# A decoder layer with 32 experts: weight reads in longer pieces, a 2 MB ring, the first token tile ahead, and a reordered tail

## The chip, the cores and the metric

The kernel runs on one core of one Trainium2 chip. The metric is device time in microseconds (us) of that core; lower is better. Several runs are taken and the median counts.

## What is computed

One layer of a hybrid decoder on 256 tokens of 1024 channels, in float32: a token mixer (gated delta rule, a linear recurrent unit and sliding-window attention, merged and projected), then 32 experts of which each token takes its top four, then a gated per-token embedding, with a layer norm after each.

```python
def moe(h, router_w, router_b, w_gu, b_gu, w_down, b_down):
    logits = (xt @ router_w + router_b).astype(jnp.float32)
    top_vals, top_idx = lax.top_k(logits, TOP_K)            # 4 of 32
    gates = jax.nn.softmax(top_vals, axis=-1)
    ...
        return clamped_swiglu(xb @ w_gu[e] + b_gu[e]) @ w_down[e] + b_down[e]
    ...

def reference(...):
        y = token_mixer(x, ...)                             # ends in (g_a*y_a + g_b*y_b + g_c*y_c) @ w_out
        x = layer_norm(DEEPNORM_ALPHA * x + y, ln1_g[i], ln1_b[i])
        y = moe(x, router_w[i], router_b[i], w_gu[i], b_gu[i], w_down[i], b_down[i])
        x = layer_norm(DEEPNORM_ALPHA * x + y, ln2_g[i], ln2_b[i])
        ple = jax.nn.sigmoid(x @ ple_w_gate[i]) * (p[i] @ ple_w_proj[i])
        x = layer_norm(DEEPNORM_ALPHA * x + ple, ln3_g[i], ln3_b[i])
```

`w_gu` is 1024 x 2048 per expert (8 MB), `w_down` 1024 x 1024 (4 MB): 384 MB in all, read once.

## The kernel before, in words

**Mixer** (to about 456 us). The work of TensorE is a list of *units*: a projection of 128 columns, or, at the end, `out_unit(c, t)`, the output projection of 256 columns (quarter `c`) for 128 tokens (tile `t`). Operands are split into a high and a low part, and a product is three matmuls (L350, L1085). Everything else (gates, recurrences, attention, norms) is written as generators, the *strands*; `run()` advances each by one `yield` per unit, and a strand may `wait` for named events. So the place of a `yield` and the order of the units set the order of instructions on each engine. After its last quarter a tile of tokens gets `first_norm(t)`: two scalar-tensor-tensor instructions per half of 512 channels (L1109, L1110), eight transposes on TensorE (L1115), copies on ScalarE, and the router's matmuls (L1122). `router()` then takes the top four per token on VectorE (L1146 to L1165), and turns them into positions.

**Experts** (`moe`). For each expert SyncE streams weights into a ring of buffers: 20 of 1 MB (8 KB per partition), of which the last eight lie in a pool `el` that the mixer shares, and are filled with the first expert's `w_gu` while the mixer ends (`prefetch`, L1037). `chunk` (L1288) reads one block of 128 rows of `w_gu`, `chunk3` (L1296) two blocks of `w_down`. A read is issued when TensorE has used up the buffer's former content. TensorE gathers the tokens of two experts at a time with one-hot matrices (`gathered`, L1358), multiplies with `w_gu` in eight steps over k (L1395, eight records a step), then VectorE and ScalarE do the clamped SwiGLU, TensorE turns it (L1423) and multiplies with `w_down` (L1431), and `spread` (L1454, L1459) adds the weighted result of the expert before to the accumulator `Y`. `mid(k)` and `fill(i)` place this other work between the steps. In expert 0 `mid` also places `residual()` (L1309): the sum of the gates times `b_down`, by two transposes (L1313) and eight matmul records (L1319), and the scaled residual as the first content of `Y`.

**Tail.** A branch for experts with more than 64 tokens (`overflow`), the second norm, the gate of the embedding (8 products over k of high and low parts, L1605, with weights split by `highs` on ScalarE and `lows` on VectorE or GpSimd, L1575), the sigmoid and product, the third norm, and the output. `moments` has a power on GpSimd (L1584) between the two instructions of a norm (L1588, L1589).

Names in the rows: `w`, `E` ring buffers, `xs` the normed tokens, `gu`, `dn`, `cb`, `pg`, `pjt` results in PSUM, `oh` one-hot matrices, `bd` and `gT` the down biases and turned gates, `mvs` mean and variance.

Of the kernel before, what the change touches and what calls it, by code (L numbers as in the profile page):

```python
# [27 lines left out]
RING = 20  # L28
EARLY = 8
# [82 lines left out]
def mixer(mx, tc, nc, a, xs, rt, dram, cst, ones, el):  # L112
# [32 lines left out]
    E = [el.tile([P, 2048], F32, name=f"E{i}", tag=f"E{i}") for i in range(4)]  # L145
# [54 lines left out]
    wg = big("E6", [P, 2, H, P])  # L200
# [4 lines left out]
    def late_parameters():  # L205
# [217 lines left out]
    M["BH"] = big("E4", [P, KD, T], F32R)  # L423
    M["BL"] = big("E5", [P, KD, T], F32R)
# [504 lines left out]
    def attend(gq, qT):  # L929
# [175 lines left out]
    def first_norm(t):  # L1105
        xT, gb = M["xT"], M["gb"]
        for hf in range(2):
            c = slice(hf * 512, (hf + 1) * 512)
            dve.scalar_tensor_tensor(xs[:, t, c], xs[:, t, c], mv[:, t, 0:1], gb[:, 0, c], ALU.subtract, ALU.mult)  # L1109
            dve.scalar_tensor_tensor(xs[:, t, c], xs[:, t, c], mv[:, t, 2:3], gb[:, 1, c], ALU.mult, ALU.add)  # L1110
        yield
        for hf in range(2):
# [5 lines left out]
            if t == 0:  # L1118
                yield
        for hf in range(2):  # L1120
            for k in range(4 * hf, 4 * hf + 4):
                pe.matmul(M["rps", t][:, :NE], xT[:, k, t * P:(t + 1) * P], rw[:, k], start=k == 0, stop=k == KD - 1)  # L1122
            if t == 0:
                yield
        yield
        events.add(f"r{t}")

    def router():

        yield from wait("r0")  # L1130
# [88 lines left out]
    for n, (t, c) in enumerate(((0, 0), (1, 0), (0, 1), (1, 1), (0, 2), (0, 3), (1, 2), (1, 3))):  # L1219
        units.append((*out_unit(c, t), (), n == 0))  # L1220
# [31 lines left out]
def moe(ctx, tc, nc, a, out, dbg, xs, rt, dram, cst, ones, el, early):  # L1252
# [53 lines left out]
    bd = w2.tile([NE, D], F32, name="bd", tag="xe")  # L1306
    pool.dma_start(bd, a["b_down"][0])

    def residual():  # L1309
        gT = w2.tile([NE, T], F32, name="gT", tag="gt")  # L1310
# [5 lines left out]
        for t in range(2):  # L1316
            for hf in range(2):
# [379 lines left out]
```

## Time and profile before

| | us |
|---|---|
| median of 3 runs (1451.98 to 1454.62) | 1453.3 |
| profiled execution | 1452.93 |
| its span, first to last instruction | 1451.2 |
| TensorE busy in the span | 1351.8 (93%) |
| VectorE, ScalarE, GpSimd busy | 608.7, 374.1, 258.9 |
| DMA: mean over the span | 332 GB/s |

The mean granted clock of TensorE is 0.981 of full speed. Busy times are sums over stages that differ, so they don't tell which engine sets the end of one; the rows below are read stage by stage.

### The profile page before, as it was taken

Reading aid. Unit: us, or ns where it says so; the run is one execution under the profiler, and the core shown is the slowest. Engines: PE = TensorE matmul, PEld = TensorE weight load, DVE = VectorE, ACT = ScalarE, POOL = GpSimd, SP = SyncE. Lnnn points to the kernel's source line nnn. Section 1 sums busy time; section 2 is a strip of 40 time slices with the busy share of each in tenths; the row PEclk is TensorE's granted clock in tenths of the full one; section 3 lists DMA queues with packets and bytes.
Section 4 is the critical chain, followed back from the end, with each engine's and each line's share of the span. In section 5 each row is a group of like instructions: output and inputs, shape, how many; then the busy total and the mean of one; then the engine's idle time right before and its main releaser. Section 6 shows DMA issues by size and latency. Waiting matters only on the chain. (4 is left out here: it accounts for less than half of the span.)

```text
span 1451.2 us, 21242 instructions
## 1 busy us (share of the span) xinstructions
PE 1351.8 (93%) x8472; PEld 781.2 (54%) x8473; DVE 608.7 (42%) x1285; ACT 374.1 (26%) x771; POOL 258.9 (18%) x221
## 2 busy tenths in 40 slices
PE   8989988999988999999999999999998989989976
PEld 7989988899988433333333333333333333333325
DVE  6497984965685222322322322222223222222257
ACT  6767464644551110110110111010101100101121
POOL 5655773534551000000000000000000000000021
PEclk9999999999998899999999999999999999999998
DMA  8754565446988699999999999999999999999960
GB/s 259 217 141 124 147 175 152 117 137 201 282 266 335 239 414 423 424 426 424 425 424 425 425 425 423 424 425 425 424 423 425 425 425 423 424 425 424 425 283 30
DMA packets 206832, 481.81 MB, mean 332 GB/s; under 512 B 13468, under 2 KB 137004, under 8 KB 174856
## 3 DMA queue, kind: packets, MB, share of 16 engines
q1 hardware_dynamic: 205128, 477.17, 84.7%
q0 software_dynamic: 848, 1.86, 0.4%
q10 hardware_dynamic: 752, 1.38, 0.3%
q8 instruction: 68, 1.11, 0.3%
q14 instruction: 36, 0.29, 0.1%
HBM read 478.78 MB, written 3.42 MB: 332 GB/s over the span
## 5 line engine op out<-in xcount | busy, mean ns | idle before, releaser
L1395 PE MATMUL gu<-w,xe 128*64 128x512 f32 x1208 | 274.8, 599 | 10.8 <-DMA w<-in_w_gu_dram 10.7
L350 PE MATMUL pjt<-xh,HI 128*128 128x256 f32 x680 | 199.0, 293 | 12.3 <-DVE cv L416 6.1
L1395 PE MATMUL gu<-E,xe 128*64 128x512 f32 x840 | 193.2, 603 | 6.7 <-DMA E<-in_w_gu_dram 6.7
L374 POOL TENSOR_TENSOR LO<-w,HI 128x384 fp32r<-128x384 f32 (+1 forms) x111 | 166.5, 1502 | 173.0 <-ACT HI L369 167.6
L350 PE MATMUL pjt<-xh,LO 128*128 128x256 f32 x680 | 193.1, 284 | 2.8 <-DVE LO L372 1.9
L350 PE MATMUL pjt<-xl,HI 128*128 128x256 f32 x680 | 193.0, 284 | 0.0
L1395 PEld LDWEIGHTS gu<-w,xe 128*64 128x64 f32 x1208 | 82.9, 137 | 177.4 <-issue 138.5
L1413 DVE TENSOR_SCALAR gc<-gu 128x256 f32<-128x256 f32 x64 | 26.9, 421 | 289.2 <-PE gu L1395 289.2
L1327 POOL DMA_DIRECT2D pt<-in_p_dram x1 | 0.8, 777 | 798.6 <-DVE lc L1417 798.6
L1431 PE MATMUL dn<-w,hT 128*64 128x512 f32 x608 | 140.5, 602 | 1.5 <-ACT hT L1424 1.5
L350 PEld LDWEIGHTS pjt<-xh,HI 128*128 128x128 f32 x680 | 130.8, 192 | 17.7 <-issue 4.3
L372 DVE TENSOR_TENSOR LO<-w,HI 128x640 fp32r<-128x640 f32 (+1 forms) x111 | 113.1, 1020 | 61.6 <-ACT HI L369 59.8
L350 PEld LDWEIGHTS pjt<-xh,LO 128*128 128x128 f32 x680 | 130.9, 192 | 3.2 <-DVE LO L372 2.1
L1459 DVE TENSOR_TENSOR Y<-Y,cb 128x512 f32<-128x512 f32 x128 | 82.1, 682 | 117.0 <-PE cb L1454 117.0
L350 PEld LDWEIGHTS pjt<-xl,HI 128*128 128x128 f32 x680 | 131.0, 193 | 0.2
L369 ACT CAST HI<-w 128x1024 fp32r<-128x1024 f32 x111 | 115.5, 1041 | 44.7 <-PE pjt L350 18.4
L1395 PEld LDWEIGHTS gu<-E,xe 128*64 128x64 f32 x840 | 57.6, 138 | 122.2 <-issue 97.9
L1414 ACT ACTIVATE sg<-gc 128x256 f32<-128x256 f32 x64 | 26.8, 419 | 298.2 <-DVE gc L1413 298.2
L1358 PE MATMUL gat<-oh,xs 128*128 128x128 f32 x512 | 75.9, 293 | 25.9 <-DVE oh L1366 19.9
L1431 PE MATMUL dn<-E,hT 128*64 128x512 f32 x416 | 95.4, 598 | 0.0
L1358 PEld LDWEIGHTS gat<-oh,xs 128*128 128x128 f32 x512 | 64.0, 196 | 47.1 <-issue 27.8
L1431 PEld LDWEIGHTS dn<-w,hT 128*64 128x64 f32 x608 | 40.4, 137 | 75.9 <-issue 64.4
(409 smaller groups left out, 1601.3 us busy)
## 6 DMA issues: line engine op xcount, KB each, us to landing
w<-in_w_gu_dram SPq DMA_DIRECT2D x151, 1024.0 KB, 19.6
E<-in_w_gu_dram SPq DMA_DIRECT2D x97, 1024.0 KB, 19.6
w<-in_w_down_dram SPq DMA_DIRECT2D x76, 1024.0 KB, 19.6
E<-in_w_down_dram SPq DMA_DIRECT2D x52, 1024.0 KB, 19.7
w<-in_w_in_dram SPq DMA_DIRECT2D x85, 512.0 KB, 3.8
E<-in_w_gu_dram SPq DMA_DIRECT2D x16, 512.0 KB, 4.8
w<-in_w_o_lru_dram SPq DMA_DIRECT2D x8, 512.0 KB, 4.6
w<-in_w_o_swa_dram SPq DMA_DIRECT2D x8, 512.0 KB, 3.9
```

Source lines behind the costliest of these rows:

```text
L350: pe.matmul(ps, hl[l][:, k], b[r][:, k], start=k == 0 and n == 0, stop=k == KD - 1 and n == 2)
L369: act.copy(hi, s)
L372: dve.tensor_sub(lo[:, 0:n], s[:, 0:n], hi[:, 0:n].bitcast(F32))
L374: pool.tensor_tensor(out=lo[:, n:], in0=s[:, n:], in1=hi[:, n:].bitcast(F32), op=ALU.subtract)
L1327: pool.dma_start(pt, a["p"][0, 0].rearrange("(t p) c -> p t c", p=P))
L1358: pe.matmul(ps[:, kk], xs[:, t, k * P:(k + 1) * P], oh[:, t], start=t == 0, stop=t == 1)
L1395: pe.matmul(gu[64 * j:64 * j + 64, b], xe[:, k], w[:, j * D + b * 512:j * D + (b + 1) * 512], start=False, stop=k == KD - 1)
L1413: dve.tensor_scalar(gc[:, c], guv[:, c, 0], 7.0, None, op0=ALU.min)
L1414: act.activation(sg[:, c], gc[:, c], AF.Sigmoid, scale=1.702)
L1431: pe.matmul(dn[64 * jj:64 * jj + 64], hT[:, 2 * hf + kk, j * 64:j * 64 + 64], w[:, kk, jj * 512:(jj + 1) * 512], start=hf == j == kk == 0, ...
L1459: dve.tensor_add(y, y, pss[jj])
```

## The change

Five things change together; line numbers in this section are those of the changed kernel where its code is meant.

1. **Layout and ring.** `w_gu` is read as "(p k) c": partition p holds rows 8p to 8p+7, so one read of 2 MB takes 16 KB in one piece per partition, with 64 KB from one partition's piece to the next. `w_down` is read as "(j h p c) d": 8 KB in one piece per partition, 1 MB per read, two reads per buffer. The ring has 10 buffers of 2 MB (16 KB per partition); four of them are prefetched. To match, the norm writes the channels of `xs` in another order (its second instruction reads with a stride of 8 elements), the router's weights are read in that order, and the turns of the SwiGLU's output take every second column. The first `spread` into each tile undoes the order, and brings the scaled residual in.
2. **Down biases** are added to `Y` in expert 22 instead of expert 0.
3. **Output projection.** Tile 0's quarters come earlier, its router matmuls stand together, and its top four are issued on VectorE behind the second tile's norm.
4. **Tail.** The gate's weights are issued from the last step of expert 31. GpSimd keeps one half block of the low parts, and VectorE does the rest. Norms are written as both first halves, then both second halves. The gate's products come in the order high-high, low-high, high-low.
5. `spread` takes its three products in another order.

```diff
-RING = 20
-EARLY = 8
+RING = 10
+EARLY = 4
...
-        for i in (0, 1, 2, 4, 5, 3, 6, 7):
...
-            t = el.tile([P, 2048], F32, name=f"E{i}", tag=f"E{i}")
...
-                sync.dma_start(t[:, c], a["w_gu"][0, 0, k * P:(k + 1) * P, c])
+        wgu = a["w_gu"][0, 0].rearrange("(p k) c -> p k c", k=KD)
+        for k, i in enumerate((0, 2, 1, 3)):
...
+            for n in range(2):
+                sync.dma_start(F[i][:, n * 2048:(n + 1) * 2048], wgu[:, 2 * k + n])
+                yield
                 yield
...
+        xc = wp.tile([P, KD, P], F32, name="xc", tag="w").rearrange("p a c -> p (a c)")
         for hf in range(2):
             c = slice(hf * 512, (hf + 1) * 512)
-            dve.scalar_tensor_tensor(xs[:, t, c], xs[:, t, c], mv[:, t, 0:1], gb[:, 0, c], ALU.subtract, ALU.mult)
-            dve.scalar_tensor_tensor(xs[:, t, c], xs[:, t, c], mv[:, t, 2:3], gb[:, 1, c], ALU.mult, ALU.add)
-        yield
+            dve.scalar_tensor_tensor(xc[:, c], xs[:, t, c], mv[:, t, 0:1], gb[:, 0, c], ALU.subtract, ALU.mult)
+        qk = lambda v, hf: v.rearrange("p (k q) -> p q k", q=KD)[:, 4 * hf:4 * hf + 4]
+        for hf in range(2):
+            dve.scalar_tensor_tensor(xs[:, t, 512 * hf:512 * hf + 512].rearrange("p (q k) -> p q k", q=4), qk(xc, hf),
+                                     mv[:, t, 2:3], qk(gb[:, 1], hf), ALU.mult, ALU.add)
...
-        yield from wait("r0")
+        yield from wait("r0", "n1")
...
-    for n, (t, c) in enumerate(((0, 0), (1, 0), (0, 1), (1, 1), (0, 2), (0, 3), (1, 2), (1, 3))):
+    for n, (t, c) in enumerate(((0, 0), (0, 1), (1, 0), (0, 2), (0, 3), (1, 1), (1, 2), (1, 3))):
...
+    def rows_up(src):
...
+                    units[k // 2] = buffer()
+                    sync.dma_start(units[k // 2], src(k // 2))
+            return units[k // 2][:, (k % 2) * 2048:(k % 2 + 1) * 2048]
...
+    def rows_down(src):
...
+                units[hf] = buffer()
+                for j2 in range(2):
+                    sync.dma_start(units[hf][:, j2 * 2048:(j2 + 1) * 2048], src(j2, hf))
...
-                dve.scalar_tensor_tensor(Y[:, t, sl], xs[:, t, sl], ALPHA, ps, ALU.mult, ALU.add)
...
+                dve.tensor_add(Y[:, t, sl], Y[:, t, sl], ps)
+                yield
...
-    wgu = a["w_gu"][0].rearrange("e (k p) c -> e k p c", p=P)
-    wdn = a["w_down"][0].rearrange("e (k p) c -> e p k c", p=P)
+    wgu = a["w_gu"][0].rearrange("e (p k) c -> e p (k c)", k=KD)
+    wdn = a["w_down"][0].rearrange("e (j h p c) d -> e j h p (c d)", j=2, h=2, c=2)
...
+                if t in fresh:
...
+                    dve.scalar_tensor_tensor(kq(y), xs[:, t].rearrange("p (q k) -> p q k", q=KD)[:, :, 64 * jj:64 * jj + 64],
+                                             ALPHA, kq(pss[jj]), ALU.mult, ALU.add)
...
-                if k == 1:
-                    next(begin)
-                if k == 3:
-                    next(begin)
-                if k == 4:
-                    next(begin, None)
+            if e == BIASED:
+                if k == 0:
+                    bias_rows.append(down_biases())
+                if k in (1, 3, 4, 5, 6):
+                    next(bias_rows[0])
...
-    lows(0, pool, slice(0, 1))
-    moments(0, 0, 2)
-    lows(0, pool, slice(1, 2))
-    for c in halves:
-        norm(0, 0, c)
...
-    lows(1, dve)
...
-    lows(2, pool)
...
-    lows(3, dve)
...
+    highs(0)
+    lows(0, pool, slice(0, 1))
     overflow()
...
+    moments(0, 0)
+    centred(0, 0, halves[0])
+    stats(1, 0)
+    scaled(0, 0, halves[0])
...
+    lows(0, dve, slice(1, 2))
+    for i in (1, 2, 3):
+        lows(i, dve)
...
+    gate(g0, 0, halves, "hl", True, False)
...
+    gate(g0, 0, halves, "w", False, True)
```

How it moves instructions, at three places. First PE at the end of the mixer, before: after the last unit come tile 0's transposes and a part of its router matmuls, between them the bias matmuls of expert 0 (L1379), then tile 1's transposes and the remaining router matmuls of both.

```order
L1115 MATMUL pg<-cst,xs 128x128 x8
L1379 LDWEIGHTS pick
L1379 MATMUL gu<-bias,pick 64x512
L1122 MATMUL pg<-rw,MG 128x32 x4
L1379 LDWEIGHTS pick
L1379 MATMUL gu<-bias,pick 64x512
L1379 LDWEIGHTS pick
L1379 MATMUL gu<-bias,pick 64x512
L1379 LDWEIGHTS pick
L1379 MATMUL gu<-bias,pick 64x512
L1115 MATMUL pg<-cst,xs 128x128 x8
L1122 MATMUL pg<-rw,MG 128x32 x12
```
PE there in the changed kernel, where the second to last unit ends and the last begins:

```order
L1091 MATMUL pjt<-RV,U 128x256
L1091 MATMUL pjt<-KT,AT 128x256
L1129 MATMUL pg<-cst,xs 128x128 x8
L1091 MATMUL pjt<-xh,AT 128x256
L1091 MATMUL pjt<-xh,U 128x256
```
and behind the last unit:

```order
L1091 MATMUL pjt<-xl,AT 128x256
L1135 MATMUL pg<-rw,MG 128x32 x8
L1403 LDWEIGHTS pick
L1403 MATMUL gu<-bias,pick 64x512
L1403 LDWEIGHTS pick
L1403 MATMUL gu<-bias,pick 64x512
L1403 LDWEIGHTS pick
L1403 MATMUL gu<-bias,pick 64x512
L1403 LDWEIGHTS pick
L1403 MATMUL gu<-bias,pick 64x512
L1129 MATMUL pg<-cst,xs 128x128 x8
L1135 MATMUL pg<-rw,MG 128x32 x8
```
Tile 0's transposes (L1129) now stand ahead of the last unit, and its router matmuls (L1135) ahead of tile 1's transposes; only tile 1's own follow.

Second, PE in the first expert, before (`E_` and `w_` with a number are ring buffers):

```order
L1358 MATMUL gat<-oh_5584,xs 128x128 x4
L1395 MATMUL gu<-E_4173,xe 64x512 x4
L1358 MATMUL gat<-oh_5584,xs 128x128 x4
L1313 MATMUL gps<-cst,GP 32x128 x2
L1395 MATMUL gu<-E_4260,xe 64x512 x4
L1401 MATMUL gwt<-cst,gw 128x128 x2
L1395 MATMUL gu<-E_4489,xe 64x512 x4
L1319 MATMUL cb<-bd,gT 128x512 x3
L1395 MATMUL gu<-E_4560,xe 64x512 x4
L1319 MATMUL cb<-bd,gT 128x512
L1395 MATMUL gu<-E_4703,xe 64x512 x4
L1395 MATMUL gu<-E_4778,xe 64x512 x4
```
and in the changed kernel:

```order
L1419 MATMUL gu<-F_97,xe 64x512 x4
L1382 MATMUL gat<-oh_5558,xs 128x128 x4
L1419 MATMUL gu<-F_97,xe 64x512 x4
L1382 MATMUL gat<-oh_5558,xs 128x128 x4
L1419 MATMUL gu<-F_4473,xe 64x512 x4
L1425 MATMUL gwt<-cst,gw 128x128 x2
L1419 MATMUL gu<-F_4473,xe 64x512 x4
L1419 MATMUL gu<-F_98,xe 64x512 x8
L1419 MATMUL gu<-F_99,xe 64x512 x8
```
L1313 and L1319 are gone from here, and two steps over k use one buffer.

Third, DVE in the tail, from tile 0's second norm on, before:

```order
L1582 BN_AGGR mvs<-bns 128x2
L1583 TENSOR_SCALAR mvs<-mvs 128x1
L1588 SCALAR_TENSOR_TENSOR Y<-Y,mvs,w_7495 128x512
L1589 SCALAR_TENSOR_TENSOR Y<-Y,mvs,w_7495 128x512
L1588 SCALAR_TENSOR_TENSOR Y<-Y,mvs,w_7495 128x512
L1589 SCALAR_TENSOR_TENSOR Y<-Y,mvs,w_7495 128x512
L1598 TENSOR_TENSOR w_10572<-tr,w_10571 128x4x128
L1575 TENSOR_TENSOR E_10303<-w_10294,E_10302 128x2048
L1598 TENSOR_TENSOR w_10572<-tr,w_10571 128x4x128
L1575 TENSOR_TENSOR E_10307<-w_10298,E_10306 128x2048
L1578 BN_STATS bns<-Y 128x6 x2
L1582 BN_AGGR mvs<-bns 128x2
```
and in the changed kernel, from the same norm's second instruction on:

```order
L1635 SCALAR_TENSOR_TENSOR Y<-Y,mvs,w_7330 128x512
L1632 SCALAR_TENSOR_TENSOR Y<-Y,mvs,w_7330 128x512
L1635 SCALAR_TENSOR_TENSOR Y<-Y,mvs,w_7330 128x512
L1623 BN_STATS bns<-Y 128x6
L1627 BN_AGGR mvs<-bns 128x2
L1628 TENSOR_SCALAR mvs<-mvs 128x1
L1645 TENSOR_TENSOR w_10215<-tr,w_10215 128x4x128 x2
L1632 SCALAR_TENSOR_TENSOR Y<-Y,mvs,w_7330 128x512 x2
L1635 SCALAR_TENSOR_TENSOR Y<-Y,mvs,w_7330 128x512 x2
L1620 TENSOR_TENSOR F_9898<-w_9890,F_9896 128x1024
L1620 TENSOR_TENSOR F_9898<-w_9890,F_9896 128x2048
L1620 TENSOR_TENSOR w_9899<-F_9893,F_9897 128x2048 x2
```
Tile 1's statistics and moments move up into tile 0's norm, its norm goes ahead of the subtractions of low parts (L1620), and there are three and a half blocks of these on DVE where there were two (L1575).

## Rows read from the trace of the kernel before

**Rows 1.** The page, parts 1 and 2: busy time; GB/s in 40 slices

```profile
PE 1351.8 (93%) x8472; PEld 781.2 (54%) x8473; DVE 608.7 (42%) x1285; ACT 374.1 (26%) x771; POOL 258.9 (18%) x221
...
GB/s 259 217 141 124 147 175 152 117 137 201 282 266 335 239 414 423 424 426 424 425 424 425 425 425 423 424 425 425 424 423 425 425 425 423 424 425 424 425 283 30
```

**Rows 2.** Stretches: PE, PEld, DVE, ACT, POOL busy, then clock, DMA share, GB/s

```profile
470.00:480.00 10.00, 9.69 (x49) 6.22 (x50) 2.17 (x13) 1.29 (x4) 0.56 (x1) 0.78 0.27 84
480.00:490.00 10.00, 10.00 (x40) 3.44 (x38) 2.48 (x4) 2.28 (x4) 0.00 (x0) 0.90 0.94 344
490.00:500.00 10.00, 7.86 (x32) 2.44 (x29) 2.92 (x8) 0.42 (x1) 0.00 (x0) 0.93 0.80 291
500.00:510.00 10.00, 9.29 (x44) 4.46 (x44) 1.29 (x4) 1.71 (x5) 0.00 (x0) 0.83 0.61 238
510.00:520.00 10.00, 10.00 (x52) 3.35 (x48) 1.63 (x4) 0.96 (x2) 0.00 (x0) 1.00 0.98 383
```

**Rows 3.** Timeline of SP's queue: start, duration, issue, count

```profile
476.62 8.73 SPq L1298 DMA_DIRECT2D E<-in_w_down_dram  x4
```

**Rows 4.** One line's instructions, L1401 on PE, in 540:900 and in 1130:1400

```profile
L1401 PE MATMUL gwt<-cst,gw x26: 272/300/328, 544.4 to 878.3; 128*128 128x128 f32 x26
...
L1401 PE MATMUL gwt<-cst,gw x18: 272/300/329, 1136.6 to 1379.0; 128*128 128x128 f32 x18
```

**Rows 5.** DMA traffic in 668.6:676.1 (w_down alone) and in 678.7:695.7 (w_gu alone)

```profile
DMA packets 817, 3.15 MB, mean 420 GB/s; under 512 B 49, under 2 KB 49, under 8 KB 816
...
DMA packets 993, 7.24 MB, mean 426 GB/s; under 512 B 110, under 2 KB 110, under 8 KB 110
```

**Rows 6.** Timeline of PE, the first expert and the start of the second

```profile
474.64 1.94 PE L1395 MATMUL gu<-E,xe 128*64 128x512 f32 x8
...
477.60 1.94 PE L1395 MATMUL gu<-E,xe 128*64 128x512 f32 x8
...
480.46 0.38 PE L1313 MATMUL gps<-cst,GP 128*32 128x128 f32 x2
480.77 1.94 PE L1395 MATMUL gu<-E,xe 128*64 128x512 f32 x8
...
484.88 2.84 PE L1319 MATMUL cb<-bd,gT 32*128 32x512 f32 x6
487.64 3.34 PE L1395 MATMUL gu<-E,xe 128*64 128x512 f32 x8
...
512.43 5.32 PE L1395 MATMUL gu<-w,xe 128*64 128x512 f32 x24
```

**Rows 7.** Timelines of PE, then DVE, at the end of the mixer

```profile
455.15 1.03 PE L1115 MATMUL pg<-cst,xs 128*128 128x128 f32 x8
...
460.64 5.08 PE L1122 MATMUL pg<-rw,MG 128*128 128x32 f32 x24
...
465.76 0.19 DVE L1146 TENSOR_TENSOR wk<-pg,small 128x32 f32<-128x32 f32 x1 [5.73 <-PE pg L1122]
...
468.38 0.18 DVE L1146 TENSOR_TENSOR wk<-pg,small 128x32 f32<-128x32 f32 x1
```

**Rows 8.** Timelines of DVE, then POOL, in the tail

```profile
1408.01 2.83 DVE L1589 SCALAR_TENSOR_TENSOR Y<-Y,mvs,w 128x512 f32<-128x512 f32 x1 [0.46 <-POOL mvs L1584]
1410.77 4.99 DVE L1588 SCALAR_TENSOR_TENSOR Y<-Y,mvs,w 128x512 f32<-128x512 f32 x1
1415.79 0.75 DVE L1589 SCALAR_TENSOR_TENSOR Y<-Y,mvs,w 128x512 f32<-128x512 f32 x1
...
1417.06 2.28 DVE L1575 TENSOR_TENSOR E<-w,E 128x2048 fp32r<-128x2048 f32 x1
...
1410.26 4.95 POOL L1575 TENSOR_TENSOR E<-w,E 128x2048 fp32r<-128x2048 f32 x1
```

**Rows 9.** Timeline of PE: last step of the experts; end of the first gate

```profile
1386.79 1.94 PE L1395 MATMUL gu<-E,xe 128*64 128x512 f32 x8 [0.52 <-DMA E<-in_w_gu_dram]
...
1429.06 1.64 PE L1605 MATMUL gu<-E,w 128*128 128x512 f32 x6
```

More of the change, by code (lines that the diff above doesn't have):

```diff
@@ L1496, in moe @@
     GRP = 2
+    BIASED = 22
+    bias_rows = []
     lnw = []
+    wgt = a["ple_w_gate"][0].rearrange("(k p) d -> p k d", p=P)
+    raws, highv, lowv, last = [], [], [], []
+    st = me.tile([P, 2, 2, 3, 6], F32, name="bns")
+    mv = me.tile([P, 2, 2, 4], F32, name="mvs")
+    halves = [slice(0, 512), slice(512, 1024)]
     prev, ahead, gather = None, [], group(0)
@@ L1502, in begun @@
         return biased(lambda q: rt.pick[:, r + q:r + q + 1], rt.bias[:, e // 8])
[L1504 removed]
+    gu, first = begun(0), gather
     next(first)
@@ L1531, in mid @@
                 next(product)
+            if e == NE - 1 and k == KD - 1:
+                got = {(j, hf): wd(j, hf) for hf in range(2) for j in range(2)}
+                last.extend([[got[j, hf] for hf in range(2)] for j in range(2)])
+                for h in hold(2):
+                    t_ = held(h, [P, 2, 2, D])
+                    for n in range(2):
+                        sync.dma_start(t_[:, n], wgt[:, 2 * len(raws):2 * len(raws) + 2])
+                        raws.append(t_[:, n])
+                for v in (highv, lowv):
+                    v.extend([t_[:, n] for t_ in [held(h, [P, 2, 2, D], F32R) for h in hold(2)] for n in range(2)])
         def fill(i):
@@ L1628, in moe @@
-    for g in first:
-        next(g)
-    next(first[0])
-    lows(1, dve)
-    next(first[1])
-    lows(2, pool)
-    highs(3)
-    lows(3, dve)
-    for hf in range(2):
-        stats(1, hf)
-    moments(1, 0, 2)
-    for c in halves:
-        norm(1, 0, c)
-    g0 = pgu.tile([P, 2, 512], F32, name="gu", tag="gu")
-    for i in range(4):
-        for hf, c in enumerate(halves):
-            if i == 3:
-                for _ in turned(1, hf):
-                    pass
-            gate(g0[:, hf], 0, c, (2 * i, 2 * i + 1))
+    moments(0, 0)
@@ L1648, in moe @@
+    gate(g0, 0, halves, "hl", True, False)
+    subs = [turned(1, hf) for hf in range(2)]
+    for f in subs:
+        f()
+    gate(g0, 0, halves, "w", False, True)
     for hf, c in enumerate(halves):
-        embed(g0[:, hf], 0, c, hf, (dve, pool)[hf])
+        embed(g0[hf], 0, c, hf)
     if "X2" in dbg:
         pool.dma_start(dbg["X2"], Y)
-    moments(0, 1, 2)
-    parts = [slice(0, 512), slice(512, 768), slice(768, 1024)]
-    gs = [p1.tile([P, 512], F32, name="cb", tag="cb", bufs=3)[:, :c.stop - c.start] for c in parts]
@@ L1655, in moe @@
-    for c in halves:
-        norm(0, 1, c)
-        sync.dma_start(out[0, 0:P, c], Y[:, 0, c])
-    for i, c in enumerate(parts):
-        gate(gs[i], 1, c, range(KD))
-        embed(gs[i], 1, c, i, (pool, dve, dve)[i])
+    moments(0, 1)
+    for i, c in enumerate((slice(0, 512), slice(512, 768), slice(768, 1024))):
+        g1 = p1.tile([P, 512], F32, name="cb", tag="cb", bufs=3)[:, :c.stop - c.start]
+        gate([g1], 1, [c], "hlw", True, True)
+        if i == 0:
+            for f in (centred, scaled):
+                for h in halves:
+                    f(0, 1, h)
+            sync.dma_start(out[0, 0:P], Y[:, 0])
+        embed(g1, 1, c, i)
@@ L1661, in moe @@
     moments(1, 1, 3)
     for c in halves:
-        norm(1, 1, c)
+        centred(1, 1, c)
+    for c in halves:
+        scaled(1, 1, c)
         sync.dma_start(out[0, P:T, c], Y[:, 1, c])
```

178 lines of the change are left out of this document (96 added, 82 removed).

## The prediction, made before the changed kernel was run

> **What bounds the kernel now.** I read the first two parts of the page first [rows 1]: PE is busy for 93% of the span, and yet from the 15th slice to the 38th the DMA engines move 414 to 426 GB/s without a break. That stretch is the 32 experts, and the stream of their weights runs through all of it. Then the stretches around its start [rows 2]: between 470 and 520 us the stream is not full. With 425 GB/s as full, it lacks 341, 81, 134, 187 and 42 GB/s over 10 us each, 7.85 MB or 18.5 us. The ring is full there, and SP issues the next weight only when the first expert has used one [rows 3]. Whatever shortens that gap, or the time per byte after it, ends the stream earlier. How far that goes shows in the spacing of the gate transposes on PE [rows 4]: they come twice per expert, so 13 experts up to 878.3 took 333.9/12 = 27.8 us each (PE alone sets that), and the nine from 1136.6 to 1379.0 took 242.4/8 = 30.3 us (the stream sets it). PE alone would therefore end about nine experts times 2.5 = 22 us sooner; up to there a gain of the stream counts in full.
>
> The sum is made against the profiled execution, 1452.9 us (span 1451.2); the median of the runs, 1453.3, is 0.4 above it. No change can be told from about 0.2%, 2.9 us.
>
> **Term 1, longer pieces per read.** A read of w_down had pieces of 4 KB and gets 8 KB, one of w_gu had 8 KB and gets 16 KB. The trace has stretches with one size alone [rows 5]: 3.15 MB in 817 packets at 420 GB/s (4 KB each, but for 49 short ones), and 7.24 MB in 993 at 426 (8 KB each, but for 110). One MB (1,048,576 bytes) takes 2.497 us at 420 and 2.461 at 426: 128 packets fewer are worth 0.036 us. For w_down's 4 MB that gives 0.14 us. No row has 16 KB; if a packet costs the same whatever its size, 64 fewer per MB are worth 0.018, so 8 MB give 0.14. Together 0.28 us per expert, times some 30 experts that are streamed after the ring is full: **−8.5**. Ends: 0, if the rate of the two stretches differs for another reason, and −13, if the difference is half again as large (the two rates are read to 1 GB/s).
>
> What speaks against it is the address pattern: a partition's next 16 KB now lie 64 KB from its neighbour's, where a read of w_gu was one solid MB before. The row for w_down is the nearest: its two pieces per partition lie 512 KB apart, and it still runs at 420. The Trainium skill (DMA: Bandwidth & Descriptors, section Latency and other measured facts) states under HBM row pitch at large powers of two that copies with a row pitch of 512 KiB ran at 207 GB/s where 214 was full, and slower at larger pitches; it has nothing for 64 KiB, and no row here shows such a pitch between partitions. If the same loss of 3% held here, the sum would come out at about 1458, an estimate from that page.
>
> **Term 2, the down biases leave expert 0.** Two transposes and eight matmuls of 512 columns go out of the first expert [rows 6], on PE, while the stream waits for PE to free buffers. By the starts on either side the transposes hold up the next step by 0.31 us and the first six matmuls by 2.76; the other two at that rate make 0.92: **−4.0**. Ends: −4.6, the two priced by more than that rate, and −3, if the next gather waits longer for it. Where they go, expert 22, the stream sets the pace: PE's 4.0 us meet 2.5 us of slack per expert [rows 4], so they are made up for within two experts; the ring is as good as empty there, so a late release delays no read. Should that cover be gone, the 4.0 come back. The four adds stay on DVE, busy for 42% of the span.
>
> **Term 3, first tile ahead.** PE's order at the end of the mixer changes: the transposes of tile 0 (1.03 us) stand before the last unit, and all 16 records of its router matmuls before tile 1's transposes; 8 of 24 were behind them (5.08/24 = 0.21 us each [rows 7]). So +1.0 and −1.7. The top four of tile 0 ran from 465.76 to 468.38 on DVE, after the last router matmul; their input is now ready before tile 1's, so these 2.6 us lie beside PE's transposes and matmuls. Tile 1's norm must have ended first, which it does (pow now under the two first halves). That makes −3.3. Against it: the second half of each norm now reads two operands with a 32-byte stride. Its price is in no row; 0.75 us is the plain one [rows 8], so I bound it by 0 and by doubling for tile 1's two, +1.5, and take the middle: **−2.5**, with ends at −3.3 and 0. The Trainium skill (SBUF — State Buffer, cachelines) states that lines are 16 bytes, with a penalty at each access that crosses to another; no run here shows it. By it the term is nearer to −1.8.
>
> SP's reads for the ring stand behind the same units of the projection as before, so the ring fills no later. The eight prefetch reads are now 1 MB instead of sixteen of 512 KB, the same bytes in the same place.
>
> **Term 4, coarser grain.** A buffer of 2 MB comes free after two steps over k, not one. The first refill was issued at 476.62 [rows 3], when the first step had ended; it now waits for the second, 2.96 us later (474.64 to 477.60 [rows 6] is one step with its gather). Later steps take 1.77 (5.32 us for three [rows 6]), so the gap grows by 1.8 to 3.0; I take 2.3. At the end the last w_gu read lands at the same time, and one step started on it at 1386.79 after a wait [rows 9]; now two steps remain: +1.8. Together **+4.1**, ends 2 and 6. Down's reads stay at 1 MB.
>
> **Term 5, the tail.** GpSimd's subtraction of 4.95 us [rows 8] goes to DVE. While it and the half block ahead of it ran, two norm instructions on DVE took 2.83 and 4.99 us instead of 0.75; without them tile 0's norm ends 2.1 + 4.2 = 6.3 us sooner. DVE then has two turned halves to subtract, tile 1's statistics and norm, and three and a half blocks of 2.28 before the last gate matmuls: 2 × 0.75 + 5 × 0.75 + 3.5 × 2.28, some 13.2 us. PE's share, 48 matmuls and the transposes of both tiles, took 14.2 us from the norm's end (1416.54) to the end of the first gate (1430.70 [rows 9]). DVE's load just fits below PE's, so I give 0.6 back: −5.7. The second tile's gate keeps its 48 matmuls. In the last norm the two first halves now lie on the pow's wait, 0.46 in the row of the first one [rows 8]: −0.4. **−6.1**, ends −8 and −1 (−1: DVE's subtractions come last). The 4 MB of gate weights are issued at the same place in SP's order, behind the last w_down, and tile 1's statistics lie under tile 0's pow.
>
> **Sum:** −8.5 − 4.0 − 2.5 + 4.1 − 6.1 = −17.0, so 1452.9 − 17.0 = **1436 us**. The stream's part, −10.9, stays within the 22 us above which PE would set the end.
>
> **Rivals.**
> - *The wide pitch slows w_gu* (slower). HBM serves 16 engines worse when partitions lie 64 KB apart, all through the experts. Without w_gu's 4.2 us the sum is −12.8; over 30 experts the point of no gain is 0.43 us per 8 MB, a rate of some 417 GB/s. Its price is in no row: between the 1.4% that part the two kinds of stretch and the 10% by which the stream was below 426 in 510:520 [rows 2], with the engines nearly full, I take 5%: 19.7 us become 20.7, +30, and 1470. For it: every read changes. The Trainium skill's rule on row pitch, named above, speaks for it too. Against it: w_down's 512 KB jumps cost nothing beyond its smaller packets.
> - *Packets beyond 8 KB, or of any size, give nothing*: 1436 + 8.5 = 1444. For it: 426 of 420 is a small difference between neighbouring stretches.
> - *The tail gives back its gain*: DVE, with 8.0 us of subtractions of which GpSimd had a part before, ends last: 1442.
> - *The ring's grain costs thrice* (12 us: each group's change stalls the stream by one step more), and packets give nothing: 1444 + 8 = 1452, no change. The same time results if the experts' gains don't reach the end.
>
> **Chances and range.** The sum as worked out 0.60 (its own range 1428 to 1442), packets nothing 0.12, tail 0.10, grain 0.07, pitch 0.11. Faster by over 0.2%: 0.82; within: 0.07; slower: 0.11. The range takes the first three, with the far end of term 1 below (4.5 us more, and with it the far ends of terms 2, 3 and 5, 0.6 + 0.8 + 1.9) and two of the failures together (packets and tail) above: 1428 to 1450. Since such bounds tend to miss what has no row, I put the lower end at 1424.
>
> **What would show it.** Right: stretches of w_gu alone at 428 to 429 GB/s, of w_down at 426; less than 16 us lacking between 470 and 520; the router and the gathers of expert 0 some 2.5 us earlier; no norm instruction in the tail above 1 us; last down matmul to the end of the span 44 us instead of 51. Wrong: w_gu below 420, PE waiting for w_gu long before 1100, subtractions last before the final gate matmuls, or norm halves of 1.5 us at the router.

## The result, and the profile of the changed kernel

The changed kernel takes 1434.4 us (median of 4 runs, 1433.1 to 1436.6) against 1452.7 us for the kernel before (4 runs): a ratio of 0.9873, interval 0.9856 to 0.9891, or 18 us less. The forecast was 1436 us. The profiled execution took 1434.1 us with a span of 1432.3, 18.9 less than the span before.

The page of the changed kernel, the line that answers to the second of [rows 1], shows the stream of weights at 426 to 430 GB/s where it ran at 423 to 426:

```profile
GB/s 257 220 134 136 128 183 159 119 132 178 262 293 327 305 416 428 427 429 427 430 426 428 428 429 428 427 430 428 428 427 427 430 429 427 428 426 430 429 330 30
```

Its stretches that answer to [rows 2] (busy time of PE, PEld, DVE, ACT, POOL, then granted clock, DMA share, GB/s):

```profile
470.00:480.00 10.00, 10.00 (x52) 6.06 (x53) 1.04 (x7) 1.49 (x4) 0.00 (x0) 0.84 0.18 56
480.00:490.00 10.00, 9.90 (x46) 3.00 (x42) 0.48 (x2) 1.66 (x2) 0.00 (x0) 1.00 1.02 424
490.00:500.00 10.00, 7.73 (x35) 4.33 (x36) 3.47 (x10) 1.75 (x5) 0.00 (x0) 0.83 0.92 393
500.00:510.00 10.00, 9.54 (x46) 3.21 (x46) 1.20 (x3) 0.96 (x2) 0.00 (x0) 1.00 0.93 360
510.00:520.00 10.00, 10.00 (x50) 3.47 (x48) 1.18 (x3) 0.67 (x2) 0.00 (x0) 1.00 0.99 419
```

Against 428 GB/s the stream lacks 372, 4, 35, 68 and 9 GB/s here, 4.9 MB or 11.4 us, where it lacked 18.5 us. What is left is mostly one hole between 470 and 480. The traffic of two long stretches, 0:520 and 520:1360, first of the kernel before and then of the changed one, gives the two parts of the stream's gain:

```profile
DMA packets 138869, 106.06 MB, mean 204 GB/s; under 512 B 7672, under 2 KB 131208, under 8 KB 136642
...
DMA packets 63685, 356.45 MB, mean 424 GB/s; under 512 B 5445, under 2 KB 5445, under 8 KB 34968
```

```profile
DMA packets 135861, 108.96 MB, mean 210 GB/s; under 512 B 7463, under 2 KB 130999, under 8 KB 132175
...
DMA packets 33062, 359.57 MB, mean 428 GB/s; under 512 B 3662, under 2 KB 3662, under 8 KB 3986
```

The changed kernel has moved 2.90 MB more by 520 us, 6.8 us at 428 GB/s, and 3.12 MB more in the next 840 us, 7.3 us. The packets of the second stretch fell from 63685 to 33062.

On PE, the timeline of the changed kernel in the router and expert 0 (answering to [rows 6, 7]):

```profile
462.11 3.46 PE L1135 MATMUL pg<-rw,MG 128*128 128x32 f32 x16
...
472.80 2.08 PE L1419 MATMUL gu<-F,xe 128*64 128x512 f32 x8
...
481.09 8.80 PE L1419 MATMUL gu<-F,xe 128*64 128x512 f32 x40
...
504.77 5.32 PE L1419 MATMUL gu<-w,xe 128*64 128x512 f32 x24
```

The first step of expert 0 begins at 472.80 instead of 474.64, and expert 1 at 504.77 instead of 512.43: 1.8 us were won ahead of expert 0 and 5.8 inside it. The same line as in [rows 4], now L1425:

```profile
L1425 PE MATMUL gwt<-cst,gw x26: 272/300/332, 536.8 to 870.0; 128*128 128x128 f32 x26
...
L1425 PE MATMUL gwt<-cst,gw x18: 272/300/332, 1128.8 to 1367.0; 128*128 128x128 f32 x18
```

Thirteen experts took 333.2/12 = 27.8 us each as before, where PE sets the pace, and the last nine 238.2/8 = 29.8 instead of 30.3. At the end of the experts and in the tail, PE and then DVE (answering to [rows 8, 9]):

```profile
1372.99 3.65 PE L1419 MATMUL gu<-w,xe 128*64 128x512 f32 x16 [0.43 <-DMA w<-in_w_gu_dram]
...
1384.48 3.65 PE L1454 MATMUL dn<-w,hT 128*64 128x512 f32 x16
...
1411.10 1.21 PE L1654 MATMUL gu<-w,w 128*128 128x512 f32 x4 [0.48 <-DVE w L1620]
```

```profile
1395.89 0.73 DVE L1635 SCALAR_TENSOR_TENSOR Y<-Y,mvs,w 128x512 f32<-128x512 f32 x1
1396.54 0.75 DVE L1632 SCALAR_TENSOR_TENSOR Y<-Y,mvs,w 128x512 f32<-128x512 f32 x1
...
1406.55 4.49 DVE L1620 TENSOR_TENSOR w<-F,F 128x2048 fp32r<-128x2048 f32 x2
```

In the kernel before, the last down matmuls stood here:

```profile
1396.43 3.65 PE L1431 MATMUL dn<-w,hT 128*64 128x512 f32 x16
```

The last down matmul ends at 1388.13 (1400.08 before), 12.0 us sooner, and from there to the end of the span it is 44.2 us instead of 51.1: 6.9 us less. The norm instructions beside which GpSimd worked (2.83 and 4.99 us before) take 0.73 and 0.75.

So the 18.9 us of the span are 1.8 ahead of expert 0, 5.8 inside it, 7.3 of the stream's rate, 6.9 in the tail, less 3.0 (rounded). The 3.0 are what PE did not get of the stream's lead: PE gained 7.7 us by expert 1 and the stream 6.8 by 520; by the end of its stretch the stream was 14.1 us ahead, and PE 12.0.

### The profile page after: what moved, and what is told of

It reads as the page before. It is cut to its first block, busy times and chain, and to the rows that moved or that the text cites. A ratio compares the mean times of both kernels' runs of the same rounds, so it can differ in the third digit from the quotient of the medians.

```text
span 1432.3 us, 20918 instructions
## 1 busy us (share of the span) xinstructions
PE 1348.4 (94%) x8472; PEld 788.8 (55%) x8473; DVE 607.2 (42%) x1289; ACT 374.6 (26%) x771; POOL 248.7 (17%) x217
## 3 DMA queue, kind: packets, MB, share of 16 engines
q0 software_dynamic: 848, 1.86, 0.4%
## 5 line engine op out<-in xcount | busy, mean ns | idle before, releaser
L1419 PE MATMUL gu<-w,xe 128*64 128x512 f32 x1168 | 262.9, 598 | 6.9 <-DMA w<-in_w_gu_dram 6.9
L1419 PE MATMUL gu<-F,xe 128*64 128x512 f32 x880 | 199.1, 596 | 5.0 <-DMA F<-in_w_gu_dram 5.0
L353 PEld LDWEIGHTS pjt<-xh,HI 128*128 128x128 f32 x680 | 131.3, 193 | 18.3 <-issue 4.7
L1454 PE MATMUL dn<-w,hT 128*64 128x512 f32 x560 | 128.5, 601 | 1.5 <-ACT hT L1447 1.5
L1419 PEld LDWEIGHTS gu<-F,xe 128*64 128x64 f32 x880 | 60.4, 137 | 119.6 <-issue 105.6
L1454 PE MATMUL dn<-F,hT 128*64 128x512 f32 x464 | 106.0, 598 | 0.0
L1382 PEld LDWEIGHTS gat<-oh,xs 128*128 128x128 f32 x512 | 64.4, 197 | 44.5 <-issue 27.8
L1427 DVE TENSOR_TENSOR gt<-gwt,gt 128x256 fp32r<-128x256 f32 x32 | 13.6, 425 | 152.2 <-ACT gt L1426 152.2
```

Of the source, the lines that this page charges most:

```text
L353: pe.matmul(ps, hl[l][:, k], b[r][:, k], start=k == 0 and n == 0, stop=k == KD - 1 and n == 2)
L1382: pe.matmul(ps[:, kk], xs[:, t, k * P:(k + 1) * P], oh[:, t], start=t == 0, stop=t == 1)
L1419: pe.matmul(gu[64 * j:64 * j + 64, b], xe[:, k], w[:, j * D + b * 512:j * D + (b + 1) * 512], start=False, stop=k == KD - 1)
L1427: dve.tensor_sub(gt[:, 1], ps, gt[:, 0].bitcast(F32))
L1454: pe.matmul(dn[64 * jj:64 * jj + 64], hT[:, 2 * hf + kk, j * 64:j * 64 + 64], w[:, kk, jj * 512:(jj + 1) * 512], start=hf == j == kk == 0, ...
```

## The experiments

Every run was also compared with the kernel before on the same chip. The medians scatter by some 2 us; one cause shows in the traces: with the same code ahead of it, expert 0 began anywhere from 472.6 us (w_down in 4 KB) to 477.8 us (last read split). So parts are judged by distances within a trace, and the time stands beside them. Where the code in between is the same, these distances hardly scatter: from the first unit's evacuation on DVE to the first step of expert 0 nine traces have 37.05 to 37.08 us, and from that step to the end of the last w_gu matmul the seven with the changed kernel's pieces and biases have 903.5 to 904.5. Expert 0 alone takes 30.8 to 32.3 us where it is unchanged, so parts inside it are known to about 1 us.

**The down biases a second time in expert 0.** The transposes and matmuls stand once more between the steps of expert 0:

```diff
             if e == 0:
                 next(first, None)
+                if k == 1:
+                    extra.append(extra_biases())
+                if k in (1, 3, 4):
+                    next(extra[0], None)
```

> The changed kernel, with the two transposes and the matmuls of the down biases done a second time in expert 0, where they stood before (the second result is written to the accumulator and overwritten, so the output is the same). Theory: they hold up PE while the stream waits for it, and they also cost clock there; from the first step of expert 0 to the first step of expert 1 the changed kernel takes 32.0 us and this one 37 to 38, and the time is 1438 to 1440. Rival 1, the work alone counts (term 2 as predicted): 36 us and 1438. Rival 2, it is hidden, and the gain in expert 0 has another source: 32 us and 1434.

Measured: 1439.1 us, ratio to before 0.9899 (0.9879 to 0.9918). PE's timeline, and one stretch of it:

```profile
475.61 1.98 PE L1436 MATMUL gu<-F,xe 128*64 128x512 f32 x8
...
485.89 2.84 PE L1360 MATMUL cb<-bd,gT 32*128 32x512 f32 x6
488.65 3.00 PE L1436 MATMUL gu<-F,xe 128*64 128x512 f32 x8
491.58 2.07 PE L1360 MATMUL cb<-bd,gT 32*128 32x512 f32 x2
493.58 6.66 PE L1436 MATMUL gu<-F,xe 128*64 128x512 f32 x24
...
514.83 5.32 PE L1436 MATMUL gu<-w,xe 128*64 128x512 f32 x24
...
1382.26 3.60 PE L1436 MATMUL gu<-w,xe 128*64 128x512 f32 x16
```

```profile
490.00:495.00 5.00, 5.00 (x10) 1.03 (x8) 0.69 (x1) 0.00 (x0) 0.00 (x0) 0.50 0.50 210
```

From the first step of expert 0 to expert 1 it is 39.2 us, against 32.0: 7.2 more, of which the instructions by their starts make 0.3 + 2.8 + 2.0. The rest goes with the clock: behind the first six matmuls (from a bias matrix of 32 rows, 32 partitions in) the granted clock is 0.50, the lower of the two levels, 1.2 GHz. The next step takes 3.00 us where one takes 1.94 [rows 6], the three at 493.58 take 6.66 where three take 5.32, and in the kernel before the step behind these matmuls stood at 3.34 [rows 6]. The theory with the clock holds; its figure, 37 to 38 us, was still too small for expert 0. The end moves by somewhat less: the last w_gu matmul ends 910.3 us after the first step of expert 0, against 903.8, and the medians differ by 4.7.

**The kernel before with this one part.** Its residual alone goes to VectorE, the biases to expert 22:

```diff
-                dve.scalar_tensor_tensor(Y[:, t, sl], xs[:, t, sl], ALPHA, ps, ALU.mult, ALU.add)
+                dve.tensor_scalar(Y[:, t, sl], xs[:, t, sl], ALPHA, None, op0=ALU.mult)
...
+            if e == 22:
+                if k == 0:
+                    bias_rows.append(down_biases())
+                if k in (1, 3, 4, 5, 6):
+                    next(bias_rows[0])
```

> The kernel before with one part of the change alone: the down biases in expert 22, and in expert 0 only the scaled residual, on VectorE. Theory (work and clock): expert 0 takes 32 us from its first step to the next expert's instead of 37.8, the stream is that much ahead, 1447. Rival 1 (the work alone): 33.4 us, 1448.5. Rival 2 (expert 22 gives it back, or the gain is the layout's): 1453.

Measured: 1447.9 us against 1454.2, ratio 0.9952 (0.9933 to 0.9970): 6.3 us by the medians, 7.0 by the ratio, with 4.4 to 9.7 in the interval.

```profile
476.60 2.59 PE L1402 MATMUL gu<-E,xe 128*64 128x512 f32 x8
...
485.40 8.80 PE L1402 MATMUL gu<-E,xe 128*64 128x512 f32 x40
...
507.43 5.32 PE L1402 MATMUL gu<-w,xe 128*64 128x512 f32 x24
...
1382.24 1.94 PE L1402 MATMUL gu<-E,xe 128*64 128x512 f32 x8 [0.49 <-DMA E<-in_w_gu_dram]
```

Expert 0 takes 30.8 us instead of 37.8, and its last five steps 8.80 without a gap. The last w_gu matmul ends 907.6 us after the first step, where it was 914.1 [rows 6, 9]: 6.5 of the 7.0 us are still there at the end. In the run above 6.4 of 7.2 were, with expert 22 unchanged, so expert 22 gives nothing back that can be seen. Both directions agree on about 7 us in expert 0, of which some 6.5 reach the end.

**The size of the pieces.** Five kernels change only how the weights are read. Edits, as the call that issues a read: two reads of 8 KB pieces with the 64 KB pitch; two solid blocks of 1 MB; w_down as before; solid blocks in one 2 MB read; w_down's 2 MB in one read.

```diff
-                    sync.dma_start(units[k // 2], src(k // 2))
+                        for n in range(2):
+                            sync.dma_start(units[k // 2][:, n * 2048:(n + 1) * 2048], one(k + n))
...
+    wgs = a["w_gu"][0].rearrange("e (k p) c -> e k p c", p=P)
...
+    wdn = a["w_down"][0].rearrange("e (j h c p) d -> e j h p c d", j=2, h=2, c=2)
...
+                      rows_up(lambda g: wgs[e, :, 2 * g:2 * g + 2]), lambda j, h: last[j][h] if last else wd(j, h), mid, fill)
...
+                sync.dma_start(units[hf].rearrange("p (j c) -> p j c", j=2), src(hf))
```

> The changed kernel, but w_gu's 2 MB in two reads of 1 MB each, with pieces of 8 KB that lie 64 KB apart. Theory (a packet has a fixed cost, the pitch none): stretches of w_gu alone at 425 to 426 GB/s instead of 430, 0.14 us more per expert, +4 us, 1438. Rival 1 (the pitch costs): below 420, 1445 and more. Rival 2 (size beyond 8 KB gives nothing): as the changed kernel, 1434.

> The changed kernel, but each 2 MB of w_gu read as two solid blocks of 1 MB with 8 KB per partition, as before. (The rows then meet other channels of the tokens, so the experts multiply the wrong pairs; the amount of work is the same.) Theory (a packet has a fixed cost, the pitch none): the same as with 8 KB pieces 64 KB apart, 425 to 426 GB/s in stretches of w_gu, 1438. Rival (the pitch costs): faster than that kernel by 3 us or more.

> The changed kernel, but w_down read in pieces of 4 KB, two per partition and read, as before, and the turn of the SwiGLU's output as before. Theory (fixed cost per packet): stretches of w_down alone at 420 GB/s instead of 426, 0.14 us more per expert, +4 us, 1438. Rival (no such cost): as the changed kernel, 1434.

> The changed kernel, with w_gu in 2 MB reads as there, but each of two solid blocks, so in pieces of 8 KB. (The rows meet other channels of the tokens, so the experts multiply the wrong pairs; the amount of work is the same.) Theory A (the number of reads sets the stream's rate between full pieces): 428 GB/s in 520:1360 as in the changed kernel, 1434. Theory B (the piece of 16 KB does): 424.7 as with 1 MB reads, 1441.

> The changed kernel, with each 2 MB of w_down in one read of two pieces of 8 KB per partition, six reads per expert instead of eight. Theory A (the number of reads counts): above 428 GB/s, 429 or more, and 2 us sooner, 1432. Theory B (only pieces count): 428.1 and 1434.

The traffic in 520:1360 of each, in this order:

```profile
DMA packets 49132, 356.80 MB, mean 425 GB/s; under 512 B 5449, under 2 KB 5449, under 8 KB 5773
```

```profile
DMA packets 49133, 356.78 MB, mean 425 GB/s; under 512 B 5453, under 2 KB 5453, under 8 KB 5777
```

```profile
DMA packets 47310, 357.09 MB, mean 425 GB/s; under 512 B 3644, under 2 KB 3644, under 8 KB 32800
```

```profile
DMA packets 47342, 356.92 MB, mean 425 GB/s; under 512 B 3644, under 2 KB 3644, under 8 KB 3968
```

```profile
DMA packets 32266, 359.64 MB, mean 428 GB/s; under 512 B 2769, under 2 KB 2769, under 8 KB 3093
```

| w_gu pieces | w_down pieces | reads per expert | MB in 520:1360 | time, us (ratio to before) |
|---|---|---|---|---|
| 8 KB solid | 4 KB | 12 | 356.45 | the kernel before |
| 8 KB, 64 KB apart | 8 KB | 12 | 356.80 | 1442.3 (0.9915) |
| 8 KB solid | 8 KB | 12 | 356.78 | 1441.1 (0.9922) |
| 8 KB solid | 8 KB | 8 | 356.92 | 1441.6 (0.9922) |
| 16 KB | 4 KB | 8 | 357.09 | 1441.3 (0.9921) |
| 16 KB | 8 KB | 8 | 359.57 | 1434.4 (0.9873), the changed kernel |
| 16 KB | 8 KB | 6 | 359.64 | 1436.3 (0.9880) |

Three things follow. With pieces of 8 KB the pitch of 64 KB costs nothing: 356.80 against 356.78 MB (16 KB pieces were not read from a solid block). The number of reads does next to nothing: 8 or 12 with 8 KB pieces, 6 or 8 with 16 KB; both runs on it came out by their theory B. And the gain isn't the sum of two: against the kernel before, longer pieces of w_down alone give 0.3 MB, of w_gu alone 0.6, both 3.1. A fixed cost per packet, as the prediction had it, would give 1.5 MB to each. Undoing either takes some 7 us by the medians (4.8 to 6.4 by the end of the last w_gu matmul), where three expectations had 4.

One kernel is missing for the sum: the changed one with both pieces short. The kernel before stands in for it, and it also differs in its ring. But the packets' own times, averaged over each trace in 520:1360, show the same. A packet of 8 KB took 309.5 ns in the kernel before, beside 4 KB ones, and 311.0 where all pieces are 8 KB; one of 4 KB took 159.2 ns in the kernel before and 160.5 beside 16 KB ones. So when one weight's pieces grow, the other's packets get longer by 1.3 to 1.5 ns, about 0.1 us per expert, of the 0.15 to 0.24 us that the growth saves. With both grown (310.4 and 614.0 ns) nothing of that shows. Why the two need each other stays open.

**GpSimd's blocks given back.**

```diff
     moments(0, 0)
+    lows(0, pool, slice(1, 2))
+    lows(2, pool)
     centred(0, 0, halves[0])
...
-    lows(0, dve, slice(1, 2))
-    for i in (1, 2, 3):
+    for i in (1, 3):
         lows(i, dve)
```

> The changed kernel, with one and a half more blocks of low parts subtracted on GpSimd while VectorE normalises tile 0, as before, and so fewer on VectorE. Theory (the two engines slow each other): two norm instructions of 3 to 5 us instead of 0.75, the first gate ends 4 to 6 us later, 1439. Rival (VectorE's load is what ends last, so less of it helps): the first gate ends 2 us sooner, 1432.

Measured: 1442.0 us, ratio 0.9914 (0.9897 to 0.9930). DVE, then POOL:

```profile
1396.95 2.77 DVE L1635 SCALAR_TENSOR_TENSOR Y<-Y,mvs,w 128x512 f32<-128x512 f32 x1
1399.64 4.99 DVE L1632 SCALAR_TENSOR_TENSOR Y<-Y,mvs,w 128x512 f32<-128x512 f32 x1
```

```profile
1399.14 4.95 POOL L1620 TENSOR_TENSOR w<-F,F 128x2048 fp32r<-128x2048 f32 x1
```

The two instructions are stretched as before, the first gate ends 31.4 us after the last down matmul instead of 24.2, and the tail is 51.2 us instead of 44.2. The theory holds, with more than its 4 to 6 us, and the rival falls: undoing this part alone takes back all that the tail had won.

**The old order of the units.**

```diff
-((0, 0), (0, 1), (1, 0), (0, 2), (0, 3), (1, 1), (1, 2), (1, 3))
+((0, 0), (1, 0), (0, 1), (1, 1), (0, 2), (0, 3), (1, 2), (1, 3))
```

> The changed kernel with the old order of the eight last units of the output projection. Theory: of the 1.8 us by which the first step of expert 0 came sooner, most came from tile 0's transposes and router matmuls standing ahead, so it comes 1 to 2 us later, and so does the end, 1436. Rival (the gain is the order of the two halves in the norm, with power hidden): no more than 0.5 us.

Measured: 1432.4 us, ratio 0.9844 (0.9824 to 0.9864). From the first unit's evacuation on DVE to the first step of expert 0, in the changed kernel (with 472.80 above) and here:

```profile
435.73 0.41 DVE L1095 SCALAR_TENSOR_TENSOR xs<-xs,pjt 128x256 f32<-128x256 f32 x1
```

```profile
438.51 0.42 DVE L1095 SCALAR_TENSOR_TENSOR xs<-xs,pjt 128x256 f32<-128x256 f32 x1
...
474.81 2.89 PE L1419 MATMUL gu<-F,xe 128*64 128x512 f32 x8
```

In the kernel before, the first unit's evacuation stood here (its first step of expert 0 at 474.64 [rows 6]):

```profile
435.88 0.41 DVE L1089 SCALAR_TENSOR_TENSOR xs<-xs,pjt 128x256 f32<-128x256 f32 x1
```

That is 37.1 us with the new order, 36.3 with the old one (36.3 too in the second run of the next group, which has the old order) and 38.8 in the kernel before. The theory falls: the new order costs 0.8 us instead of winning 1 to 2. The rival's bound (no more than 0.5 us won by the order) stands. What was won must then come from the other edits there, the norm's order with the power hidden and the top four behind it among them; none of them was tested by itself.

**The last read in two.** The last 2 MB of w_gu as two reads; then the same with the old unit order and the embedding's product in expert 29 instead of 30.

```diff
+                    if one is not None and k == KD - 2:
+                        for n in range(2):
+                            sync.dma_start(units[k // 2][:, n * 2048:(n + 1) * 2048], one(k + n))
...
-            if e == NE - 2 and k in (3, 5, 7):
+            if e == NE - 3 and k in (3, 5, 7):
                 next(product)
```

> The changed kernel with the last 2 MB of the last expert's w_gu in two reads of 1 MB. Theory (the coarse grain costs a step at the end): PE starts the seventh step when the first half has landed, and the last down matmul comes 1.2 to 1.8 us sooner; 1432.8. Rival (the end hangs on the last read anyway, by its landing): no gain, 1434.4.

> The changed kernel with the old order of the last units, the embedding's product in expert 29 instead of 30, and the last 2 MB of w_gu in two reads. Theory (the split alone gained nothing because the product's matmuls in expert 30 had put PE behind the stream by then): PE waits for w_gu in expert 31 again, the last w_gu matmul ends 1.2 to 1.8 us sooner after the first step of expert 0 than the changed kernel's 903.8, and with 0.8 from the order the time is 1432. Rival (PE is behind for another reason): 903.8 as it was, 1433.6.

Measured: 1434.1 us (0.9861) and 1432.9 us (0.9857, 0.9833 to 0.9880). The seventh step of expert 31 in the first; in the second it stands alike at 1375.52, also with 3.60:

```profile
1378.65 3.60 PE L1423 MATMUL gu<-w,xe 128*64 128x512 f32 x16
```

The wait of 0.43 us that stood before this step is gone, and no more: the end of the last w_gu matmul comes 904.4 and 903.4 us after the first step of expert 0, against 903.8. Both theories fall. PE, it seems, reaches the step at its own pace when the read has almost landed, in either place of the product. So the last read's grain is worth half a microsecond at most.

**PE's wait at the router filled.** Twelve more bias matmuls, overwritten by the real ones:

```diff
+        for n in range(warm):
+            c = col(n % 4)
+            pe.matmul(gu[64 * (n % 2):64 * (n % 2) + 64, n // 2 % 2], c.to_broadcast([c.shape[0], SLOTS]), rows, start=True, stop=True)
```

> The changed kernel, with twelve more bias matmuls of 512 columns (each overwritten by the real ones) put ahead of those of expert 0, into PE's wait of 1.85 us for the second tile's norm; they last about 1.9 us. Theory (it is the wait that takes PE to the lower clock level, where it stays for the router's matmuls, the gathers and the start of expert 0): the granted clock is 1.0 until the transposes at least, tile 1's 16 router records take 1.9 us instead of 3.5, the first step of expert 0 comes 2 to 4 us sooner after the first unit than the 37.1 us of the changed kernel, and the time is 1431 to 1433. Rival (the router's narrow matmuls and the later waits take the clock down anyway): 37.1 us, 1434.4, or later by what the added matmuls overrun.

Measured: 1435.3 us, ratio 0.9864 (0.9839 to 0.9890). First DVE's first evacuation, then PE; and the stretches:

```profile
438.47 0.42 DVE L1095 SCALAR_TENSOR_TENSOR xs<-xs,pjt 128x256 f32<-128x256 f32 x1
...
458.62 1.86 PE L1135 MATMUL pg<-rw,MG 128*128 128x32 f32 x16
460.42 1.49 PE L1402 MATMUL gu<-bias,pick 96*64 96x512 bf16 x12
...
464.43 2.26 PE L1135 MATMUL pg<-rw,MG 128*128 128x32 f32 x16
...
473.92 2.99 PE L1422 MATMUL gu<-F,xe 128*64 128x512 f32 x8
```

```profile
462.00:464.00 2.00, 1.00 (x9) 0.48 (x6) 1.97 (x4) 0.43 (x1) 0.00 (x0) 1.00 0.96 410
464.00:466.00 2.00, 2.00 (x18) 2.00 (x18) 1.30 (x10) 0.96 (x3) 0.00 (x0) 0.96 0.97 418
466.00:468.00 2.00, 1.54 (x8) 1.41 (x7) 0.88 (x6) 0.00 (x0) 0.00 (x0) 0.50 1.09 467
472.00:474.00 2.00, 2.00 (x12) 1.77 (x12) 0.19 (x1) 0.37 (x1) 0.00 (x0) 0.50 0.79 317
```

The clock stays at 1.0 through the transposes and falls during the router's 16 narrow matmuls, so these take 2.26 us instead of 3.46. The first step of expert 0 comes 35.4 us after the first evacuation, 1.6 sooner than in the changed kernel, where 2 to 4 were expected. Behind the router's matmuls the clock is 0.50 all the same, up to 474 us at least. So half of the theory holds, and the time (1435.3, not 1431 to 1433) can't tell the 1.6 us. What takes the clock down there stays open: the wait was not filled whole (PE is busy for 1.00 of the 2.00 us in 462:464), and sixteen matmuls of the same shape at 458.62 took 1.86 us, without a fall.

No kernel of these is clearly ahead of the changed one: the intervals of the best two, 0.9824 to 0.9864 and 0.9833 to 0.9880, overlap its own.

## Why the prediction was right, and where its steps were not

The sum, −17.0, came out at −18.3 in the medians and −18.9 in the spans. Its terms did not come out equally well: by the parts of the span, terms 2, 4 and 5 came out better than forecast by 1.8, 1.1 and 0.8 us, terms 1 and 3 worse by 1.2 and 0.7. That the sum is this close is in part luck.

Of the signs that were named, these came: 11.4 us lacking between 470 and 520 (less than 16), no norm instruction of the tail above 1 us, 44.2 us from the last down matmul to the end, and w_gu alone at 430 GB/s (702:718 and 730:746; 428 to 429 named). w_down alone, at 429 and 415 in two stretches of 7.5 us (690:697.5 and 718:725.5), can't tell 426, and the first step of expert 0 came 1.8 us sooner, not 2.5. One sign of being wrong came, without harm: DVE's subtractions ended last before the last matmuls of the first gate.

- **Term 1, longer pieces:** −8.5 forecast, 7.3 us in the stretch 520:1360. The size was right and the reason only in part: the gain is there only with both longer pieces, so the step that prices each weight's packets by themselves (0.036 and 0.018 us per MB) failed: one alone gave 0.3 or 0.6 of the 3.1 MB. The rival of the wide pitch falls (w_gu alone ran at 430 GB/s); the Trainium skill's figure for larger pitches (DMA: Bandwidth & Descriptors, Latency and other measured facts) has no counterpart at 64 KiB in these runs.
- **Term 2, biases:** −4.0 forecast; 7 us measured in expert 0 from both directions, 6.5 at the end. The changed kernel itself gained 5.8 there, with a granted clock of 0.83 in 490:500. The step that failed is "by the starts on either side": it counted the bias work's own time, and not the slower steps behind it, although the 3.34 us of one stood in [rows 6].
- **Term 3, first tile ahead:** −2.5 forecast, 1.7 measured from the first evacuation (38.8 to 37.1). Its +1.0 for tile 0's transposes ahead of the last unit held: the unit order costs 0.8. The rest, −1.7, −2.6 and +0.75, was −3.5 in sum and came out at −2.5 (38.8 to 36.3 with the old order); the +0.75 was 0.9, and which of the other two was too large, no run shows. The strided reads cost what lay inside the bounds, by the groups of DVE at the router:

```profile
L1120 DVE SCALAR_TENSOR_TENSOR xs<-xc,mv,TG 128x512 f32<-128x512 f32 x4 | 4.5, 1176 | 0.2
L1117 DVE SCALAR_TENSOR_TENSOR xc<-xs,mv,TG 128x512 f32<-128x512 f32 x4 | 2.8, 746 | 0.0
```

That is 1176 ns against 746 for the plain form, so 0.9 us per tile; the bound was 1.5, the middle 0.75. The Trainium skill's rule on lines of 16 bytes (SBUF — State Buffer, cachelines) agrees in its direction.
- "So the ring fills no later" failed, without harm: SP issued the ring's w_gu reads at 449.49, 5 us later than before (the stretch 440:450 moved 211 GB/s), but the ring was full before expert 0 began in both kernels.
- **Term 4, grain:** +4.1 forecast, 3.0 measured. At the start the first refill waits for the second step, as forecast:

```profile
477.88 6.00 SPq L1321 DMA_DIRECT2D F<-in_w_down_dram  x4
```

That is 5.1 us after the first step of expert 0, where it was 2.0 [rows 3, 6]: 3.1 later (2.96 forecast). But the stream gained only 0.9 us less than PE there (2.3 forecast). To the end 2.1 us of its lead are lost (1.8 forecast), but not at the last read, as the run with the split shows; that they are lost at each wait for 2 MB, where 1 MB was waited for, is argued and not shown.
- **Term 5, tail:** −6.1 forecast, 6.9 measured, by the mechanism named: two stretched norm instructions. DVE's subtractions end with PE's last products, as "just fits" had it: PE waits 0.48 us for them at 1411.10.

## What to carry to other kernels

Look at the stage in which a transfer waits for compute, and take out of it what can be done anywhere else: two transposes and eight matmuls that were 4 us long cost 7 there, and nothing that could be seen in expert 22. Price an instruction by the ones that follow it too, since its neighbours' durations show a lowered clock or a shared port. And when a profile suggests a cost per packet, change one stream and then both: here each alone gave little of what the two gave together.

## What the runs showed of the hardware

- TensorE's clock fell while it was busy: behind six matmuls with 32 rows of weights the granted clock was 0.50 (1.2 GHz) in 490:495, with PE busy for all of it, and one step took 3.00 us instead of 1.94. With these matmuls gone from expert 0 in the kernel before, the last five steps there took 8.80 us, 1.76 each.
- Two instructions of VectorE with two inputs in SBUF went from 0.75 to 2.8 and 5.0 us beside GpSimd's subtractions, each time (before, and with GpSimd's blocks given back). The Trainium skill (SBUF — State Buffer, Who interferes with whom) has a rule for this: such instructions block on a shared port while GpSimd reads. The trace agrees: the second one lasted 4.99 us beside a subtraction of 4.95 that had begun 0.5 us before it, and ended 0.5 us behind it, in both traces.
- The rate of the stream went from 424 to 428 GB/s only with pieces of 16 and 8 KB together; with one of the two longer it was 425.
